# A four-layer decoder trunk on one core: norm weights as columns, norm scratch inside the mixers' memory, one unit of query weights kept for both tiles

## The chip, the cores and the metric

The kernel runs on one core of a Trainium2 chip. A core has a matrix engine (TensorE, PE in the profile), a vector engine (VectorE, DVE), an activation engine (ScalarE, ACT), a general engine (GpSimd, POOL) and a queue engine (SyncE, SP), all with their own instruction streams, and 16 DMA engines between HBM and the on-chip memory (SBUF). TensorE writes to a small accumulator memory (PSUM), in banks of 128 x 512 float32. The metric is the device time of one execution in microseconds. Everything is float32.

## The reference, cut to what matters

256 tokens of width 1024 pass four layers. Each layer adds a token mixer (HGRN2, forgetting attention, Mamba-2 SSD, HGRN2) and then a PEER feed-forward: a product-key lookup that picks, for each token and each of 8 heads, 16 of 16384 experts, reads one row of `u` and one of `v` for each, and sums.

```python
def rmsnorm(x, g, eps=NORM_EPS):
    y = x * lax.rsqrt(jnp.mean(x * x, axis=-1, keepdims=True) + eps)
    return y * g

for i in range(DEPTH):
    h = h + mixer[i](rmsnorm(h, norm_mix[i]))
    h = h + peer_ffn(rmsnorm(h, norm_ffn[i]), peer_w_q[i], peer_keys[i], peer_u[i], peer_v[i])
return rmsnorm(h, norm_final)

def peer_ffn(xb, w_q, sub_keys, u_tab, v_tab):            # a block of 128 tokens
    q = (xb @ w_q).reshape(M, 8, 2, 128)                  # 16 score blocks, top 16 of each, top 16 of the sums
    ...
    act = gelu(einsum('md,mhkd->mhk', xb, u_tab[idx])) * gates
    return einsum('mhk,mhkd->md', act, v_tab[idx])
```

So there are eight norms of 256 tokens with weights of their own before mixers and feed-forwards, and a ninth at the end. `norm_ffn(h)` is used twice: for the queries, and for the products with the gathered `u` rows.

## The kernel before, in words

The tokens are two tiles of 128 (t = 0, 1), so that a layer and a tile make a stage: STAGES = 8. The expert part of stage s runs together with the mixer, the norms and the queries of stage s + 1 ("side work").

**The expert part.** A stage has 64 steps (loop `for i in range(64 * s, 64 * s + 64)`). A step takes two gathers, each an indirect DMA issued by POOL (L1096 in `fetch`) that brings 128 rows of 2048 floats (u and v of one expert, 8 KB) into one of eight buffers `GB` in the tile `arena`. `dot` multiplies the u half with `XR` on DVE and sums it, `spread` makes a gelu and diagonal weights `dg` on ACT, and TensorE adds the v half into `acc` (L1125). After that the buffer is free and POOL may issue the gather eight places further on. `XR` holds the normed tokens 64 at a time, each twice down the partitions; `repeated` makes it once per stage, with four matmuls against a selection matrix `sel` (at step 62), which ACT and DVE copy out of PSUM at step 63 (L1204, L1213, `copy` beside it).

**The side work** is a generator that gives out pieces, one piece in a step, as long as a count of estimated cost lies under SIDE[s] times the step's number over 56. Its weights come in units of 128 x 2048 floats (1 MB) through three buffers `raw`. `load_to` (L267) puts the loads on SP in the order of use, up to three units ahead, and a load waits until TensorE is done with the unit that held its buffer. A stage with HGRN2 uses 20 units, attention 16, SSD 32, and each stage then 8 units of query weights `wq`. The second tile of a layer loads all units again.

**The norm** (`normed`): ACT squares and sums, DVE and ACT make the reciprocal root r, DVE computes `xn = h * r * nw` (in `scale`), TensorE turns `xn` into `xT` (features on partitions; helper `turn`, L237) and ACT copies it from PSUM (L405). `nw` is one row of 1024 weights, copied to all 128 partitions by a DMA on SP (`norm_load`, L251): 512 KB on the chip's side. The next row is loaded in `scale`, after the last use of the row before. `xn` and `nw` are regions of `arena` of their own.

**Helpers.** Matmuls are recorded under L233 (`mm`) and L237 (`turn`), all DVE work of the wrapper `vec` under L198, activations under L211. One float32 matmul in the code is two records of TensorE in the profile.

Of the kernel before, what the change touches and what calls it, by code (L numbers as in the profile page):

```python
# [9 lines left out]
F32 = mybir.dt.float32  # L10
# [4 lines left out]
OP = mybir.AluOpType  # L15
AX = mybir.AxisListType

P = 128
T = 256
D = 1024  # L20
DC = D // P
DEPTH = 4
EPS = 1e-6
UNIT = 2048
# [4 lines left out]
NRAW = 3  # L29
MIX = 14560  # L30
STAGES = 2 * DEPTH
KIND = ("hg", "fox", "ssd", "hg")

SIDE = (37.8, 34.6, 37.5, 100, 100, 38.6, 38.4, 1.8)
# [57 lines left out]
def _cols(v):  # L92
    return np.ascontiguousarray(v.reshape(-1, P).T)
# [12 lines left out]
def _layout(x, norm_mix, norm_ffn, norm_final, hgrn_lb_logits, hgrn_w_in, hgrn_gnorm, hgrn_w_out,  # L106
            fox_w_in, fox_b_f, fox_w_out, ssm_w_in, ssm_conv_w, ssm_conv_b, ssm_dt_bias, ssm_a_log,
            ssm_d, ssm_gnorm, ssm_w_out, peer_w_q, peer_keys, peer_u, peer_v):
    a = {}
    a["x"] = np.ascontiguousarray(x.reshape(2, P, D))  # L110
    a["norms"] = np.ascontiguousarray(np.concatenate([norm_mix, norm_ffn, norm_final[None]], axis=0))

    def cols(w, *cuts):
        return np.concatenate([w[:, c * 512:(c + 1) * 512] for c in cuts], axis=1)

    for j in range(2):

        a[f"hg{j}"] = np.concatenate([_in_units(cols(hgrn_w_in[j], 2, 3, 0, 1, 4, 5, 6, 7)), _out_units(hgrn_w_out[j])])

    w = fox_w_in[0]  # L120
    a["fox"] = np.concatenate([_in_units(cols(w, 4, 5, 0, 2, 1, 3)), _out_units(fox_w_out[0])])

    w2 = ssm_w_in[0]
    a["ssm"] = np.concatenate([_in_units(cols(w2, 8, 10, 4, 5, 9, 11, 6, 7, 0, 1, 2, 3)), _out_units(ssm_w_out[0])])
    for i in range(DEPTH):
        a["wq%d" % i] = _in_units(peer_w_q[i])

    def small(m):
        m = np.concatenate([m, np.zeros((m.shape[0], 32 - m.shape[1]), m.dtype)], axis=1)
        return np.ascontiguousarray(m.reshape(DC, P, 32).transpose(1, 0, 2)).reshape(P, DC * 32)  # L130

    a["keys"] = np.ascontiguousarray(peer_keys.transpose(0, 4, 1, 2, 3)).reshape(DEPTH, P, UNIT)
    a["uv"] = np.concatenate([peer_u.reshape(-1, D), peer_v.reshape(-1, D)], axis=1)
    a["gn"] = np.ascontiguousarray(hgrn_gnorm)
    parts = [
        ("wf", small(w[:, 3072:3088])), ("wdt", small(w2[:, 6144:6176])),
        ("lbl", np.ascontiguousarray(hgrn_lb_logits.reshape(DEPTH, 8, P).transpose(2, 1, 0)).reshape(P, 32)),
        ("bf", _rows(fox_b_f[0])), ("dtb", _rows(ssm_dt_bias[0])), ("alog", _rows(ssm_a_log[0])),
        ("cw", np.ascontiguousarray(ssm_conv_w[0].reshape(4, 32, P).transpose(2, 1, 0)).reshape(P, 128)),
        ("cb", _cols(ssm_conv_b[0])), ("sg", _cols(ssm_gnorm[0])),  # L140
        ("sd", _cols(np.repeat(ssm_d[0], 64))),
    ]
    off = 0
    for name, arr in parts:
        PARAMS[name] = (off, arr.shape[1])
        off += arr.shape[1]
    a["par"] = np.ascontiguousarray(np.concatenate([q for _, q in parts], axis=1))
    a["const"] = _constants()
    for name in ("hg0", "fox", "ssm"):
        UNITS[name[:3].rstrip("0")] = a[name].shape[0]  # L150
    return a
# [8 lines left out]
def trunk(ctx: ExitStack, tc: tile.TileContext, d: dict, out: bass.AP):  # L160
    nc = tc.nc
    SB = bass.MemoryType.PSUM
    cpool = ctx.enter_context(tc.tile_pool(name="c", bufs=1))
# [8 lines left out]
    npar = sum(n for _, n in PARAMS.values())  # L172
    cst = cpool.tile([P, ncst], F32, name="cst")
    par = cpool.tile([P, npar], F32, name="par")
    sizes = (("h", 2 * D), ("xn", D), ("nw", D), ("xT", D), ("XR", 2 * D), ("keys", UNIT), ("SS", 2048), ("mix", MIX),
             ("gb", NGB * 2 * D))
    arena = cpool.tile([P, sum(n for _, n in sizes)], F32, name="arena")
    at_, o_ = {}, 0
# [1 line left out]
        at_[name] = arena[:, o_:o_ + n]  # L180
        o_ += n
    h = at_["h"].rearrange("p (t n) -> p t n", t=2)
    xn, nw = at_["xn"], at_["nw"]
    xT = at_["xT"].rearrange("p (c t) -> p c t", c=DC)
    XR = at_["XR"].rearrange("p (g n) -> p g n", g=2)
    keys = at_["keys"].rearrange("p (g k) -> p g k", g=16)
# [2 lines left out]
    mix = at_["mix"]  # L189
# [11 lines left out]
    vec = Vector()  # L201
# [15 lines left out]
    def PR(name):  # L217
        o, n = PARAMS[name]
        return par[:, o:o + n]
# [4 lines left out]
    spare = cpool.tile([P, 1], F32, name="spare")  # L224
    trimask = cpool.tile([P, 4, P], U8, name="trimask")
    m64 = cpool.tile([P, 64], F32, name="m64")
    sel = cpool.tile([P, 2, 2, 64], F32, name="sel")

    pe = [0.0]

    def mm(o, w, m, start, stop):
        pe[0] += max(0.27, 0.0017 * m.free_size())
        nc.tensor.matmul(o, w, m, start=start, stop=stop)  # L233
# [13 lines left out]
    def bank():  # L247
        return psp.tile([P, 512], F32, name="ps")

    def norm_load(row):  # L250
        nc.sync.dma_start(nw, d["norms"][row:row + 1].to_broadcast([P, D]))  # L251


    stream = []
    for l in range(DEPTH):
        nm = ("hg%d" % (l // 3), "fox", "ssm", "hg%d" % (l // 3))[l]
        for t in range(2):
            stream += [(nm, i) for i in range(UNITS[KIND[l] if KIND[l] != "ssd" else "ssm"])]
            stream += [("wq%d" % l, i) for i in range(8)]
    raws = {}  # L260
    pos = [0, 0]

    def load_to(n):
        while pos[0] < min(n, len(stream)):
            nm, i = stream[pos[0]]
            r = rawp.tile([P, UNIT], F32, name="raw")
            nc.sync.dma_start(r, d[nm][i])  # L267
            raws[pos[0]] = r
            pos[0] += 1

# [50 lines left out]
    def slot(*fs):  # L321
        for f in fs:
            f()
        yield
        flush()
        yield
# [33 lines left out]
    def turned(src, use, n=4):  # L360

        b = bank().rearrange("p (c t) -> p c t", c=4)
        for c in range(n):
            turn(b[:, c], src[:, c * P:(c + 1) * P])
        later(lambda: use(b))


    def normed(t, acc, row, to_x=True, alone=False):

        st = wk2.tile([P, 4], F32, name="st")  # L370
        es = [slice(e * 512, (e + 1) * 512) for e in range(2)]
        r = st[:, 2:3]

        def add(e):
            tm(h[:, t, es[e]], acc[e], h[:, t, es[e]], op=OP.add)

        def square(e):
            act(xn[:, es[e]], h[:, t, es[e]], AF.Square, accum_out=st[:, e:e + 1])

        def root():  # L380
            tm(r, st[:, 0:1], st[:, 1:2], op=OP.add)
            act(r, r, AF.Sqrt, scale=1.0 / D, bias=eps)

        def scale():
            assert rows.pop(0) == row
            vec.reciprocal(r, r)
            for e in range(2):
                stt(xn[:, es[e]], h[:, t, es[e]], r, nw[:, es[e]], op0=OP.mult, op1=OP.mult)
                if not to_x:
                    nc.sync.dma_start(out[t * P:(t + 1) * P, es[e]], xn[:, es[e]])  # L390
            if rows and rows[0] != row:
                norm_load(rows[0])

        both = [lambda e=e: square(e) for e in range(2)]
        if acc is not None:
            adds = [lambda e=e: add(e) for e in range(2)]
            if alone:
                yield from slot(lambda: deferred.extend(adds))
            else:
                both = [adds[0], both[0], adds[1], both[1]]  # L400
        yield from slot(lambda: deferred.extend(both))
        for f in (root, scale):
            yield from slot(lambda: later(f))
        if to_x:
            yield from slot(*(lambda q=q: turned(xn[:, es[q]], lambda b: nc.scalar.copy(xT[:, 4 * q:4 * q + 4], b))  # L405
                              for q in range(2)))


    def hgrn(l, t, carry):
# [669 lines left out]
    def repeated():  # L1079

        todo = []
        for g in range(2):
            for e in range(2):
                b = bank()
                mm(b, sel[:, g].rearrange("p j i -> p (j i)"), xn[:, e * 512:(e + 1) * 512], True, True)
                todo.append((XR[:, g, e * 512:(e + 1) * 512], b))
        return todo

# [42 lines left out]
    def ready(s, acc):  # L1131

        l, t = s // 2, s % 2
        carry = {}
        yield from normed(t, acc, l, alone=True)
        if t == 0:
            nc.sync.dma_start(keys, d["keys"][l].rearrange("p (g k) -> p g k", g=16))
        yield from mixers[KIND[l]](l, t, carry)
        yield from normed(t, carry["acc"], DEPTH + l)
        yield from queries(s)  # L1140

    def side(s):

        if s + 1 < STAGES:
            yield from ready(s + 1, accs.pop(s - 1) if s else None)
        else:
            yield from normed(0, accs.pop(s - 1), 2 * DEPTH, False, alone=True)


    nc.sync.dma_start(h[:, 0], d["x"][0])  # L1150
    nc.sync.dma_start(cst, d["const"])
    nc.sync.dma_start(par, d["par"])
    nc.vector.memset(eps, EPS)
    rows = [r for s in range(STAGES) for r in (s // 2, DEPTH + s // 2)] + [2 * DEPTH] * 2
    first = ready(0, None)
    norm_load(rows[0])
    for _ in range(2):
        next(first)
    load_to(NRAW)
    nc.sync.dma_start(h[:, 1], d["x"][1])  # L1160
    nc.vector.tensor_copy(trimask, tri[:, None, :].to_broadcast([P, 4, P]))
    tm(m64, ident[:, 0:64], ident[:, 64:P], op=OP.add)
    for g in range(2):
        nc.vector.tensor_copy(sel[:, g], ident[:, None, g * 64:g * 64 + 64].to_broadcast([P, 2, 64]))
    while (0, 0) not in scored:
        next(first)
    while (0, 0) not in got:
# [6 lines left out]
    for s in range(STAGES):  # L1174
# [51 lines left out]
        others()  # L1226
        for _ in work:
            pass
    for _ in normed(1, accs.pop(STAGES - 1), 2 * DEPTH, False):
        pass  # L1230


# [13 lines left out]
```

## Time and profile before

| | us |
|---|---|
| median of 3 runs (3303.47 to 3305.14) | 3303.48 |
| the profiled execution, its own time | 3302.7 |
| its span, first to last instruction | 3300.7 |
| TensorE / VectorE / ScalarE / GpSimd busy | 2500.2 / 2109.8 / 1368.9 / 1182.8 |

The span is cut into 40 slices of 82.5 us in the page. A digit of a slice is the busy share in tenths, GB/s what all DMA queues moved in it. Queue q0 carries the gathers that POOL issues, queue q1 all that SP issues. TensorE's busy time is modelled, so that its share is no measure of how near to its limit it is.

### The profile page before, as it was taken

The page shows a single profiled execution, that of the slowest core. Times are in us where ns is not written, and L with a number is a line of the kernel's source. Part 1 is how long each engine was busy: PE and PEld are TensorE (multiplying, and loading weights), DVE is VectorE, ACT ScalarE, POOL GpSimd, SP SyncE. Part 2 cuts the span into 40 slices and gives each one's busy share as a digit, 9 for nine tenths or more (in the row PEclk, how much of TensorE's full clock was granted, in tenths as well). Part 3 has the DMA queues.
Part 4 walks back from the last instruction along what each step waited for, and adds up shares of the span by engine and source line. Part 5 has one row for each costly group of instructions (what it writes and reads, how often), then busy time and mean ns, then how long its engine had stood idle before and what let it go on. Part 6 is the DMA issues. An engine that isn't in the chain of part 4 may idle for free.

```text
span 3300.7 us, 30061 instructions
## 1 busy us (share of the span) xinstructions
PE 2500.2 (76%) x8202; PEld 1090.8 (33%) x8202; DVE 2109.8 (64%) x5545; ACT 1368.9 (41%) x3911; POOL 1182.8 (36%) x1030
## 2 busy tenths in 40 slices
PE   8887776777677776788877897878777787775555
PEld 4433332332333332343333453323333333332222
DVE  1367657576565756688656886576665666567764
ACT  3254333254243533476334674244443543333332
POOL 0133334334343334333333333343333333344442
PEclk9989988898889898999988998889988898888777
DMA  7799999999999999999999999999999999999998
GB/s 269 268 421 421 421 421 420 421 411 420 418 410 421 392 421 421 421 421 419 415 419 409 419 419 417 419 411 421 418 414 413 416 420 420 414 406 412 419 415 331
DMA packets 186645, 1343.88 MB, mean 407 GB/s; under 512 B 20720, under 2 KB 20976, under 8 KB 24176
## 3 DMA queue, kind: packets, MB, share of 16 engines
q0 software_dynamic: 147456, 1073.81, 78.8%
q1 hardware_dynamic: 39024, 268.17, 19.9%
q8 instruction: 68, 1.11, 0.1%
q14 instruction: 97, 0.79, 0.1%
HBM read 1340.84 MB, written 1.05 MB: 407 GB/s over the span
## 4 chain that ended last, share of the span: by engine, by line
DMA 57%; PE 17%; issue 9%; DVE 9%; ACT 4%; POOL 3%; POOLq 0%; SPq 0%; DVEq 0%; ACTq 0%
DMA arena<-in_uv,ix 56%; PE acc L1125 9%; DVE arena L198 8%; PE pj L233 5%; POOL arena L1096 3%; PE ps L233 3%; ACT dots L211 2%; ACT L211 1%; ACT dg L211 1%; PE ps L237 1%; ACT arena L211 0%; DVE ti L198 0%; DMA raw<-in_wq 0%; DVE eq L198 0%; DVE ts L198 0%
## 5 line engine op out<-in xcount | busy, mean ns | idle before, releaser
L198 DVE SCALAR_TENSOR_TENSOR arena<-arena 128x1024 f32<-128x1024 f32 (+3 forms) x1282 | 1321.4, 1047 | 976.2 <-DMA arena<-in_uv,ix 930.1
L1096 POOL DMA_INDIRECT arena<-in_uv,ix x1024 | 1180.7, 1153 | 2090.8 <-PE acc L1125 1524.7
L1125 PE MATMUL acc<-arena,dg 128*64 128x512 f32 x4096 | 1315.1, 728 | 765.2 <-ACT dg L211 748.3
L1125 PEld LDWEIGHTS acc<-arena,dg 128*64 128x64 f32 x4096 | 484.8, 155 | 1405.9 <-ACT dg L211 1065.3
L233 PE MATMUL pj<-raw,arena 128*128 128x512 f32 x1920 | 905.9, 615 | 5.5 <-DMA raw<-in_wq 1.5
L211 ACT ACTIVATE dots<-dots 128x2 f32<-128x2 f32 x512 | 103.5, 202 | 1663.7 <-DVE arena L198 1662.6
L233 PEld LDWEIGHTS pj<-raw,arena 128*128 128x128 f32 x1920 | 355.0, 195 | 566.9 <-issue 552.8
L211 ACT ACT_TABLE_LOAD x326 | 418.3, 1283 | 5.8 <-PEq L1238 0.7
L211 ACT ACTIVATE dg<-m,dots 128x64 f32<-128x64 f32 x1024 | 292.5, 333 | 0.0
L211 ACT ACTIVATE dots<-dots,gs 128x1 f32<-128x1 f32 x1024 | 245.6, 286 | 16.8
L233 PE MATMUL ps<-arena 128*128 128x128 f32 (+5 forms) x1040 | 127.5, 284 | 1.4 <-ACT arena L972 1.4
L233 PEld LDWEIGHTS ps<-arena 128*128 128x128 f32 (+3 forms) x1040 | 103.0, 166 | 74.9 <-issue 55.6
L237 PE MATMUL ps<-cst,arena 128*128 128x128 f32 x560 | 93.1, 296 | 19.5 <-DVE arena L198 16.2
L237 PEld LDWEIGHTS ps<-cst,arena 128*128 128x128 f32 x560 | 68.7, 151 | 99.3 <-issue 36.1
L211 ACT ACTIVATE arena<-arena 128x512 f32<-128x512 f32 (+3 forms) x132 | 67.7, 555 | 44.4 <-DVE arena L198 41.7
L198 DVE DVE_READ_ACCUMULATOR arena<-arena 128x1 f32 x1024 | 83.7, 82 | 0.0
L233 PE MATMUL ps<-cst,arena 128*128 128x128 f32 (+3 forms) x352 | 74.2, 344 | 0.0
L198 DVE MAX8 sv<-arena 128x8 f32<-128x128 f32 x256 | 61.6, 282 | 13.9 <-ACT arena L981 13.9
L198 DVE FIND_INDEX8 si<-sv,arena 128x8 uint32<-128x128 f32 x256 | 69.7, 284 | 0.0
L211 ACT ACTIVATE arena<-ps 128x512 f32<-128x512 f32 (+4 forms) x113 | 46.5, 458 | 28.3 <-PE ps L233 27.7
L233 PEld LDWEIGHTS ps<-cst,arena 128*128 128x128 f32 x352 | 50.4, 193 | 22.9 <-issue 13.3
L198 DVE COPY gs<-ig 64x16 f32<-64x16 f32 x256 | 54.3, 212 | 4.7
(102 smaller groups left out, 1101.7 us busy)
## 6 DMA issues: line engine op xcount, KB each, us to landing
raw<-in_hg SPq DMA_DIRECT2D x80, 1024.0 KB
raw<-in_wq SPq DMA_DIRECT2D x64, 1024.0 KB
raw<-in_ssm SPq DMA_DIRECT2D x64, 1024.0 KB
raw<-in_fox SPq DMA_DIRECT2D x32, 1024.0 KB
arena<-in_uv,ix POOLq DMA_INDIRECT x1024
arena<-in_norms SPq DMA_DIRECT2D x17, 512.0 KB
arena<-in_keys SPq DMA_DIRECT2D x4, 1024.0 KB
arena<-in_x SPq DMA_DIRECT2D x2, 512.0 KB
```

What stands on the lines that cost most here:

```text
L198: return getattr(nc.vector, name)(o, *a, **k)
L211: nc.scalar.activation(o, i, f, **k)
L233: nc.tensor.matmul(o, w, m, start=start, stop=stop)
L237: nc.tensor.transpose(o, i, ident)
L1096: nc.gpsimd.indirect_dma_start(GB[n % NGB], None, d["uv"], bass.IndirectOffsetOnAxis(ap=got[s, hh][0][:, g, q:q + 1], axis=0))
L1125: nc.tensor.matmul(accs[s][e][g * 64:g * 64 + 64], dg[:, g], v, start=hh == 0 and q == 0, stop=hh == 7 and q == NQ - 1)
```

## The change

1. The rows of weights of the eight inner norms are laid out as 8 columns each (feature on partition) in the parameter tile `par`, which grows from 832 to 896 columns. `norm_load` is gone. DVE computes `xn = h * r` alone, and the weights are multiplied in when the turned norm leaves PSUM: a DVE multiplication with a broadcast column (`weighed`) in place of ACT's copy. The final norm keeps a row of weights, loaded once into the mixers' memory.
2. `xn` no longer has a region of its own; it lies in a part of the mixers' memory `mix` that is not in use at the time of a norm (`FREE`).
3. Since `xn` now lacks the weights, `repeated` makes `XR` from `xT`: for each of four banks, eight matmuls with 64 columns of `xT` as the stationary operand and the identity as the moving one.
4. The first unit of each layer's `wq` goes to a region `kept` (as large as `xn` and `nw` were together) and is loaded for the first tile alone.

```diff
+NKEPT = 1
+FREE = {"hg": 0, "fox": 64 + 8 * T + 2 * D, "ssd": 352 + 16 * T + 96 + D}
...
-    sizes = (("h", 2 * D), ("xn", D), ("nw", D), ("xT", D), ("XR", 2 * D), ("keys", UNIT), ("SS", 2048), ("mix", MIX),
+    sizes = (("h", 2 * D), ("xT", D), ("XR", 2 * D), ("keys", UNIT), ("SS", 2048), ("mix", MIX), ("kept", NKEPT * UNIT),
...
-    def norm_load(row):
-        nc.sync.dma_start(nw, d["norms"][row:row + 1].to_broadcast([P, D]))
...
             nm, i = stream[pos[0]]
-            r = rawp.tile([P, UNIT], F32, name="raw")
-            nc.sync.dma_start(r, d[nm][i])
+            keep = nm[0] == "w" and i < NKEPT
+            r = at_["kept"][:, i * UNIT:(i + 1) * UNIT] if keep else rawp.tile([P, UNIT], F32, name="raw")
+            if not keep or (nm, i) not in kept:
+                nc.sync.dma_start(r, d[nm][i])
+            if keep:
+                kept.add((nm, i))
...
         def scale():
-            assert rows.pop(0) == row
             vec.reciprocal(r, r)
             for e in range(2):
-                stt(xn[:, es[e]], h[:, t, es[e]], r, nw[:, es[e]], op0=OP.mult, op1=OP.mult)
-                if not to_x:
+                if last:
+                    stt(xn[:, es[e]], h[:, t, es[e]], r, row[:, es[e]], op0=OP.mult, op1=OP.mult)
                     nc.sync.dma_start(out[t * P:(t + 1) * P, es[e]], xn[:, es[e]])
-            if rows and rows[0] != row:
-                norm_load(rows[0])
-
+                else:
+                    vec.tensor_scalar(xn[:, es[e]], h[:, t, es[e]], r, None, op0=OP.mult)
+
+        def weighed(q, b):
+            c = slice(4 * q, 4 * q + 4)
+            tm(xT[:, c], b, PR("nw")[:, 8 * row + 4 * q:8 * row + 4 * q + 4].unsqueeze(2).to_broadcast([P, 4, P]), op=OP.mult)
...
-            yield from slot(*(lambda q=q: turned(xn[:, es[q]], lambda b: nc.scalar.copy(xT[:, 4 * q:4 * q + 4], b))
-                              for q in range(2)))
+            yield from slot(*(lambda q=q: turned(xn[:, es[q]], lambda b: weighed(q, b)) for q in range(2)))
...
                 b = bank()
-                mm(b, sel[:, g].rearrange("p j i -> p (j i)"), xn[:, e * 512:(e + 1) * 512], True, True)
+                for c in range(4):
+                    for j in range(2):
+                        mm(b[j * 64:j * 64 + 64, c * P:(c + 1) * P], xT[:, 4 * e + c, g * 64:g * 64 + 64], ident, True, True)
```

The order of SP's queue at the program's start and through the first layer, before (`in_norms` are the rows of norm weights, `in_hg` and `in_wq` the units):

```order
L1152 DMA par<-in_par 128x832
L251 DMA arena<-in_norms 128x1024
L267 DMA raw<-in_hg 128x2048 x3
L1160 DMA arena<-in_x 128x1024
L251 DMA arena<-in_norms 128x1024
L1137 DMA arena<-in_keys 128x2048
```

and now:

```order
L1165 DMA par<-in_par 128x896
L270 DMA raw<-in_hg 128x2048 x3
L1171 DMA arena<-in_x 128x1024
L1149 DMA arena<-in_keys 128x2048
```

Further on in the same queue, the end of the first layer's first tile and its whole second tile, before:

```order
L267 DMA raw<-in_wq 128x2048 x3
L251 DMA arena<-in_norms 128x1024
L267 DMA raw<-in_wq 128x2048 x5
L267 DMA raw<-in_hg 128x2048 x3
L251 DMA arena<-in_norms 128x1024
L267 DMA raw<-in_hg 128x2048 x17
L267 DMA raw<-in_wq 128x2048 x3
L251 DMA arena<-in_norms 128x1024
L267 DMA raw<-in_wq 128x2048 x5
```

and now, with `arena<-in_wq` the load into `kept`:

```order
L270 DMA arena<-in_wq 128x2048
L270 DMA raw<-in_wq 128x2048 x7
L270 DMA raw<-in_hg 128x2048 x20
L270 DMA raw<-in_wq 128x2048 x7
```

The loads of norm weights are gone, the second tile loads seven units of `in_wq` where it loaded eight, and the other loads stand in the same order.

On TensorE, the change from one stage's expert part to the next (here the first one; `acc` are the experts' sums), before:

```order
L1125 MATMUL acc<-arena,dg 64x512 x28
L233 MATMUL ps<-arena,sel 128x512 x4
L1125 MATMUL acc<-arena,dg 64x512 x20
```

and now:

```order
L1136 MATMUL acc<-arena,dg 64x512 x28
L235 MATMUL ps<-cst,arena 64x128 x32
L1136 MATMUL acc<-arena,dg 64x512 x20
```

The four matmuls of `repeated` have become 32, at the same place in the queue.

On DVE, the first norm that runs beside experts (second layer-one tile), before:

```order
L198 RECIPROCAL st<-st 128x1
L198 SCALAR_TENSOR_TENSOR arena<-arena,st 128x512 x2
L198 SCALAR_TENSOR_TENSOR arena,dots<-arena 128x1024 x2
L198 TENSOR_TENSOR eq<-cst,af 128x512
L198 TENSOR_TENSOR eq<-eq,sf 128x512
L198 TENSOR_REDUCE af<-eq 128x32
L198 TENSOR_SCALAR sf<-af 128x16
L198 TENSOR_TENSOR ig<-sf,af 128x16
L198 SCALAR_TENSOR_TENSOR arena,dots<-arena 128x1024 x2
```

and now:

```order
L201 RECIPROCAL st<-st 128x1
L201 TENSOR_SCALAR arena<-arena,st 128x512 x2
L201 SCALAR_TENSOR_TENSOR arena,dots<-arena 128x1024 x2
L201 TENSOR_TENSOR eq<-cst,af 128x512
L201 TENSOR_TENSOR eq<-eq,sf 128x512
L201 TENSOR_REDUCE af<-eq 128x32
L201 TENSOR_SCALAR sf<-af 128x16
L201 TENSOR_TENSOR ig<-sf,af 128x16
L201 TENSOR_TENSOR arena<-ps,par 128x512 x2
L201 SCALAR_TENSOR_TENSOR arena,dots<-arena 128x1024 x2
```

The scaling has one tensor operand in place of two, and two multiplications out of PSUM stand behind it, ahead of the next two products with gathered rows.

## Rows read from the trace of the kernel before

**Rows 1.** The page: engines, 40 slices, DMA queues.
```profile
PE 2500.2 (76%) x8202; PEld 1090.8 (33%) x8202; DVE 2109.8 (64%) x5545; ACT 1368.9 (41%) x3911; POOL 1182.8 (36%) x1030
...
DMA  7799999999999999999999999999999999999998
GB/s 269 268 421 421 421 421 420 421 411 420 418 410 421 392 421 421 421 421 419 415 419 409 419 419 417 419 411 421 418 414 413 416 420 420 414 406 412 419 415 331
...
q0 software_dynamic: 147456, 1073.81, 78.8%
q1 hardware_dynamic: 39024, 268.17, 19.9%
```

**Rows 2.** The page, the chain that ended last, by engine.
```profile
DMA 57%; PE 17%; issue 9%; DVE 9%; ACT 4%; POOL 3%; POOLq 0%; SPq 0%; DVEq 0%; ACTq 0%
```

**Rows 3.** Windows: stretch, length, busy time of each engine, granted clock, DMA share, GB/s.
```profile
140.00:540.00 400.00, 299.41 (x972) 128.20 (x970) 252.64 (x672) 161.00 (x454) 145.72 (x126) 0.89 1.01 421
...
940.00:1330.00 390.00, 290.18 (x1004) 130.19 (x1006) 256.54 (x685) 160.12 (x483) 150.85 (x130) 0.90 1.00 413
...
2970.00:3280.00 310.00, 182.28 (x491) 71.11 (x492) 206.64 (x505) 93.57 (x346) 135.45 (x122) 0.79 1.01 416
```

**Rows 4.** Waits: engine, line, waited for, us in total, times, longest.
```profile
POOL arena L1096 <- PE acc L1125: 1524.7, 441, 18.4
...
DVE arena L198 <- DMA arena<-in_uv,ix: 930.1, 559, 8.2
```

**Rows 5.** DMA issues by line: names, count, size of each.
```profile
raw<-in_wq SPq DMA_DIRECT2D x64, 1024.0 KB
...
arena<-in_norms SPq DMA_DIRECT2D x17, 512.0 KB
```

**Rows 6.** SP in order of time, 100 to 180 us: start, length, line, names.
```profile
111.41 0.33 SPq L251 DMA_DIRECT2D arena<-in_norms  x1
...
174.00 0.33 SPq L251 DMA_DIRECT2D arena<-in_norms  x1
```

**Rows 7.** The chain of the first 40 us in order of time: start, length, what.
```profile
2.13 6.94 DMA arena<-in_norms
...
9.20 0.76 DVE arena L198
...
24.28 7.36 DMA raw<-in_hg
```

**Rows 8.** VectorE in order of time, 0 to 12 us; idle time ahead in brackets.
```profile
7.54 0.16 DVE L198 RECIPROCAL st<-st 128x1 f32<-128x1 f32 x1 [0.36 <-ACT st L211]
9.20 1.41 DVE L198 SCALAR_TENSOR_TENSOR arena<-arena,st 128x512 f32<-128x512 f32 x2 [1.49 <-DMA arena<-in_norms]
```

**Rows 9.** Groups by shape: count, busy us, mean ns of one, idle before, releaser.
```profile
L198 DVE SCALAR_TENSOR_TENSOR arena<-arena,st 128x512 f32<-128x512 f32 x36 | 25.4, 748 | 2.2 <-DMA arena<-in_norms 1.5
L198 DVE TENSOR_TENSOR arena<-ps,arena 128x512 f32<-128x512 f32 x16 | 10.9, 683 | 20.2 <-PE ps L237 20.2
L198 DVE TENSOR_SCALAR arena<-arena,fst 128x256 f32<-128x256 f32 x16 | 5.2, 370 | 0.3
L198 DVE TENSOR_SCALAR arena<-arena,fst 128x128 f32<-128x128 f32 x16 | 3.9, 283 | 0.3
```

**Rows 10.** TensorE in order of time, three stretches.
```profile
2960.30 3.92 PE L1125 MATMUL acc<-arena,dg 128*64 128x512 f32 x8 [1.05 <-ACT dg L211]
2964.15 3.98 PE L233 MATMUL ps<-arena,sel 128*128 128x512 f32 x8
...
2973.37 2.17 PE L1125 MATMUL acc<-arena,dg 128*64 128x512 f32 x8 [3.27 <-ACT dg L211]
...
1519.99 0.44 PE L233 MATMUL ps<-arena 128*64 128x128 f32 x4
...
41.66 0.60 PE L237 MATMUL ps<-cst,arena 128*128 128x128 f32 x4
```

**Rows 11.** VectorE and GpSimd at the last change of stage.
```profile
2968.16 0.69 DVE L198 COPY arena<-ps 128x512 f32<-128x512 f32 x1 [3.94 <-PE ps L233]
...
2983.62 1.23 DVE L198 SCALAR_TENSOR_TENSOR arena<-arena 128x1024 f32<-128x1024 f32 x1 [1.28 <-DMA arena<-in_uv,ix]
...
2971.50 1.64 POOL L1096 DMA_INDIRECT arena<-in_uv,ix  x1 [0.30 <-issue]
```

**Rows 12.** Windows around the last change of stage, columns as in rows 3.
```profile
2960.00:2970.00 10.00, 9.70 (x24) 3.93 (x24) 4.35 (x8) 3.19 (x11) 3.03 (x4) 0.76 0.98 367
2970.00:2980.00 10.00, 4.45 (x17) 1.86 (x16) 9.97 (x31) 2.48 (x11) 5.72 (x5) 1.00 0.94 348
```

More of the change, by code (lines that the diff above doesn't have):

```diff
@@ L110, in _layout @@
     a["x"] = np.ascontiguousarray(x.reshape(2, P, D))
-    a["norms"] = np.ascontiguousarray(np.concatenate([norm_mix, norm_ffn, norm_final[None]], axis=0))
+    a["last"] = np.ascontiguousarray(norm_final[None])
     def cols(w, *cuts):
@@ L141, in _layout @@
         ("sd", _cols(np.repeat(ssm_d[0], 64))),
+        ("nw", np.concatenate([_cols(v) for v in (*norm_mix, *norm_ffn)], axis=1)),
     ]
@@ L182, in trunk @@
     h = at_["h"].rearrange("p (t n) -> p t n", t=2)
-    xn, nw = at_["xn"], at_["nw"]
     xT = at_["xT"].rearrange("p (c t) -> p c t", c=DC)
@@ L226, in trunk @@
     m64 = cpool.tile([P, 64], F32, name="m64")
-    sel = cpool.tile([P, 2, 2, 64], F32, name="sel")
     pe = [0.0]
@@ L260, in trunk @@
     raws = {}
+    kept = set()
     pos = [0, 0]
@@ L365, in turned, with normed @@
         later(lambda: use(b))
-    def normed(t, acc, row, to_x=True, alone=False):
+    def normed(t, acc, row, xn, alone=False):
         st = wk2.tile([P, 4], F32, name="st")
@@ L384, in scale @@
         def scale():
-            assert rows.pop(0) == row
             vec.reciprocal(r, r)
             for e in range(2):
-                stt(xn[:, es[e]], h[:, t, es[e]], r, nw[:, es[e]], op0=OP.mult, op1=OP.mult)
-                if not to_x:
+                if last:
+                    stt(xn[:, es[e]], h[:, t, es[e]], r, row[:, es[e]], op0=OP.mult, op1=OP.mult)
                     nc.sync.dma_start(out[t * P:(t + 1) * P, es[e]], xn[:, es[e]])
-            if rows and rows[0] != row:
-                norm_load(rows[0])
+                else:
[3 more added lines that the diff above has]
+            tm(xT[:, c], b, PR("nw")[:, 8 * row + 4 * q:8 * row + 4 * q + 4].unsqueeze(2).to_broadcast([P, 4, P]), op=OP.mult)
+        last = not isinstance(row, int)
         both = [lambda e=e: square(e) for e in range(2)]
@@ L403, in normed @@
             yield from slot(lambda: later(f))
-        if to_x:
-            yield from slot(*(lambda q=q: turned(xn[:, es[q]], lambda b: nc.scalar.copy(xT[:, 4 * q:4 * q + 4], b))
-                              for q in range(2)))
+        if not last:
+            yield from slot(*(lambda q=q: turned(xn[:, es[q]], lambda b: weighed(q, b)) for q in range(2)))
     def hgrn(l, t, carry):
@@ L1134, in ready @@
         carry = {}
-        yield from normed(t, acc, l, alone=True)
+        xn = mix[:, FREE[KIND[l]]:FREE[KIND[l]] + D]
+        yield from normed(t, acc, l, xn, alone=True)
         if t == 0:
@@ L1138, in ready @@
         yield from mixers[KIND[l]](l, t, carry)
-        yield from normed(t, carry["acc"], DEPTH + l)
+        yield from normed(t, carry["acc"], DEPTH + l, xn)
         yield from queries(s)
@@ L1146, in side @@
         else:
-            yield from normed(0, accs.pop(s - 1), 2 * DEPTH, False, alone=True)
+            nc.sync.dma_start(mix[:, 0:D], d["last"].to_broadcast([P, D]))
+            yield from normed(0, accs.pop(s - 1), mix[:, 0:D], mix[:, D:2 * D], alone=True)
     nc.sync.dma_start(h[:, 0], d["x"][0])
@@ L1153, in trunk @@
     nc.vector.memset(eps, EPS)
-    rows = [r for s in range(STAGES) for r in (s // 2, DEPTH + s // 2)] + [2 * DEPTH] * 2
     first = ready(0, None)
-    norm_load(rows[0])
     for _ in range(2):
@@ L1162, in trunk @@
     tm(m64, ident[:, 0:64], ident[:, 64:P], op=OP.add)
-    for g in range(2):
-        nc.vector.tensor_copy(sel[:, g], ident[:, None, g * 64:g * 64 + 64].to_broadcast([P, 2, 64]))
     while (0, 0) not in scored:
@@ L1228, in trunk @@
             pass
-    for _ in normed(1, accs.pop(STAGES - 1), 2 * DEPTH, False):
+    for _ in normed(1, accs.pop(STAGES - 1), mix[:, 0:D], mix[:, 2 * D:3 * D]):
         pass
```

## The prediction, made before the changed kernel ran

> **What bounds the kernel now.** I read the slices of the page first. The busiest engine, TensorE, shows 76%, but from the third slice to the last but one the DMA engines stand at 9 and move 392 to 421 GB/s [rows 1]. The windows by stage say it more finely: DMA share 1.00 or 1.01 in the first, the weakest and the last stage, at 421, 413 and 416 GB/s [rows 3]. The last of them loads almost no weights, so gathers alone fill the DMA engines nearly as well as gathers mixed with weights. Then the chain: 57% of the span is DMA [rows 2]. The waits fit: VectorE waits 930 us for gathered rows, and POOL waits 1525 us for TensorE to free a buffer [rows 4]. The latter looks like a limit by buffers, but POOL refills a queue that is not empty: a gather issued at 2971.50 is first used at 2983.62 [rows 11], 12 us later, and one gather of 1.05 MB at 420 GB/s takes 2.5 us; so four to five gathers are in the queue. Hence from about 140 us, when that state begins, to 3280 us the time is bytes over rate, and a byte not moved is time saved. Outside that stretch the first 140 us count by their own chain, and the tail of some 20 us is not touched.
>
> **The bytes.** The page counts 17 loads of norm rows at 512 KB (0.524 MB) and 64 units of query weights at 1024 KB (1.049 MB) [rows 5]. SP's first three norm loads fall before 140 us, the third at 111.41; the fourth is at 174.00 [rows 6]. So 14 lie in the full stretch; one load for the final norm is added there, which leaves 13 x 0.524 = 6.82 MB. Of the query weights the second tile of each layer loads one unit less: 4 x 1.049 = 4.19 MB; SP's order shows just that, and no load that comes instead. Together 11.01 MB. At 417 GB/s, between the stages' 413 and 421, that is 26.4 us (26.2 at 421, 26.7 at 413). `par` grows by 128 x 64 x 4 bytes, 0.03 MB, under 0.1 us.
>
> **The start.** The chain begins with the first norm row: issued at 2.13, 6.94 us [rows 7]. VectorE has its reciprocal at 7.70 (7.54 + 0.16) and then stands 1.49 us for that row [rows 8]. Without it the scaling starts 1.5 us earlier. Behind it TensorE runs on the first units until it waits for a unit whose load takes 7.36 us from 24.28 on [rows 7]. Two norm rows, 1.05 MB or 2.5 us of DMA, no longer lie ahead of that unit. So TensorE comes 1.5 us earlier and the unit up to 2.5 us earlier. I take 2 us; the ends are 0 (something behind, such as the first routing, absorbs it) and 3.5 (both add up).
>
> **VectorE and ScalarE in the norms.** There are 16 inner norms. Each drops two scalings of 748 ns and gets two with one tensor operand. The trace has these at 128 x 128 and 128 x 256, at 283 and 370 ns [rows 9]; 87 ns for 128 more columns gives some 545 ns at 512 (an estimate). It also gets two multiplications from PSUM at 683 ns [rows 9]. That is 2 x (545 + 683 - 748) = 0.96 us more per norm, 15 us in all, on an engine busy for 2110 of 3301 us and waiting 930 us for gathers; ScalarE loses two copies per norm. What stands behind the two multiplications in VectorE's queue are two products with gathered rows; they start up to 1.4 us late, and a buffer comes free that much later, against 12 us of queued gathers. I count 0; if nothing covered it, 15 us. The estimate of cost that paces the side work rises by under 1% (its formula counts a piece by TensorE or VectorE, whichever is more, and at least 0.5), so the side work keeps its steps.
>
> **The change of stage.** `repeated` now takes 64 records of 128 columns in place of 8 of 512. Before, they took 3.98 us at the last change, and VectorE stood 3.94 us for the last bank [rows 10, 11], with the products of the next stage behind it. What 64-column matmuls cost is seen in the SSD mixer: four records of 128 columns, two matmuls into the two halves of the partitions, take 0.44 us end to end [rows 10]; that is not a pace yet, since the last record drains in it. Bounds: if the halves do not overlap, 64 records at the pace of turns (four in 0.60 us with the drain, so at most 0.15 each) take up to 9.6 us; if they overlap fully, 32 times 0.11 (3.98/8/4, a quarter of the old record plus drain) gives 3.5 us, about what it was. The nearest row is the pair of the same shape: 16 pairs at 0.3 to 0.44 us, 5 to 7 us. So the copy to `XR` comes 1 to 3 us later at each of the seven changes that run beside gathers. The DMA queue's 12 us hide this, but not wholly: around the change the rate already dips, 367 and 348 GB/s at shares of 0.98 and 0.94 [rows 12]. I take 0.3 us each, 2 us in all; ends 0 and 7 x 5.7 = 40.
>
> At this place the Trainium skill has a rule (TensorEngine Tiling (Array Packing), Theoretical Speedup): a stationary operand of at most 64 columns lets two such matmuls run side by side, up to twice as fast. The row of the SSD pair agrees in part: four records took less than four turns, 0.44 against 0.60 us. By that rule at its best the term would be 0 and the sum 2 us lower.
>
> **Sum.** 3302.7 - 26.4 - 2 + 0 + 2 = 3276.3 us for an execution like the profiled one. The median of the runs lies 0.8 us above that one's own time, so 3277 us.
>
> **Rivals.**
> (a) *Paced by buffers.* If POOL's wait for TensorE [rows 4] is what limits in the stretches without weights, a norm load that falls there used DMA time that nobody else takes. For it: the dip to 348 GB/s [rows 12] and 413 GB/s in the attention stage [rows 3]. Against it: shares of 1.00 and more over whole stages. If half of the bytes saved bring nothing, the gain of 26.4 halves: 3277 + 13 = 3290 us.
> (b) *VectorE blocks POOL.* POOL issues every gather, and 32 scalings with a single tensor operand on VectorE are new. If each held POOL up for its whole 0.545 us and that showed, 32 x 0.545 = 17 us come back: 3294 us. Against it: POOL is busy for 36% [rows 1] and runs 12 us ahead. The Trainium skill names this mechanism (SBUF — State Buffer, Who interferes with whom): a one-source float32 operation on SBUF may take the port that GpSimd needs to write descriptors, and GpSimd then waits for its end. No row here shows such a wait.
> (c) *Slower: the change of stage runs the DMA queue dry.* The mechanism is the 64 records at half the clock. The eight records of the experts' sums take 3.92 us at 2960.30 and 2.17 at 2973.37 [rows 10], with a granted clock of 0.76 and 1.00 in the windows around them [rows 12], so nearly such a factor occurs. Without overlap they would take 2 x 9.6 = 19 us, 15 more than now; all seven would cost 107 us if nothing hid them. It decides when more than 28/7 = 4 us per change show, so only if the delay passes 12 + 4 us, which needs the slow end of both bounds. With 6 us shown at each, 3277 - 2 + 42 = 3317 us.
> (d) *More than the bytes.* If the dips of the rate stem from the norm rows among the gathers, up to 10 us more go: 3267 us.
> That the loads stay is excluded by SP's order.
>
> **How the numbers follow.** Forecast 3277: 0.76. (a) 0.12, (b) 0.04, (c) 0.04, (d) 0.04. The likeliest case's own range is 3270 to 3285 (start 0 to 3.5, change of stage 0 to 8, rate). For 8 in 10 I go to 3266 below, which takes in (d), and to 3292 above, which takes in most of (a). About 0.2%, 6.6 us, is what a measurement of this kernel tells from no change; faster by more is under 3296.9 us. Forecast, (a), most of (b) and (d) are there: 0.91. Within it lie the rest of (b) and the mild half of (c): 0.05. Slower 0.04.
>
> **What would show it.** DMA bytes 12.5 MB lower (1343.9 to 1331.3), the share still 9 in all slices but the ends, the rate within 410 to 421, and the last gather some 26 us earlier: each step right. The stages' lengths should shrink by 2.6 to 5.0 us in second-tile mixers' stages (two norm rows and a unit) and 2.5 us in the others. The first scaling should start at about 7.7 us. Wrong: `repeated` over 7 us with a DMA share under 0.9 behind it (c); a lower rate in stretches without weights (a); POOL's spans longer beside the new scalings (b).

## The result, and the profile after

The changed kernel takes 3275.1 us (median of 6 runs, 3273.0 to 3277.48) against 3303.6 us (6 runs, 3302.36 to 3305.14): the ratio is 0.9914, 95% interval 0.9901 to 0.9926. The forecast was 3277 us. The profiled execution lies at the upper end of its runs, 3277.4 us, 2.3 us above their median. The two traces differ by some 25 us and the medians by 28.5, so what is read from the traces below accounts for 25 us; where the other 3 lie is not shown (the start, below, is a candidate).

The page of the changed kernel, the lines that answer to [rows 1] and [rows 2]:

```profile
span 3275.6 us, 30941 instructions
...
PE 2498.5 (76%) x8650; PEld 1114.0 (34%) x8650; DVE 2116.8 (65%) x5575; ACT 1354.9 (41%) x3879; POOL 1181.0 (36%) x1030
...
DMA  7699999999999999999999999999999999999998
GB/s 259 249 421 421 421 421 420 421 414 417 420 405 421 415 417 418 413 420 416 408 420 406 421 420 407 420 412 421 417 418 417 404 421 421 420 409 419 416 414 338
DMA packets 183769, 1331.40 MB, mean 406 GB/s; under 512 B 20400, under 2 KB 20656, under 8 KB 21808
...
q1 hardware_dynamic: 36144, 255.61, 19.1%
...
DMA 58%; PE 13%; DVE 11%; issue 10%; ACT 4%; POOL 3%; POOLq 0%; DVEq 0%; ACTq 0%
```

Engines and gather queue are as they were. Queue q1 moves 255.61 MB where it moved 268.17, and the DMA digits are still 9 from the third slice on. Windows by stage, columns as in [rows 3] (the last stage is moved by the time won):

```profile
140.00:540.00 400.00, 305.11 (x978) 129.74 (x976) 254.70 (x677) 160.60 (x453) 143.95 (x128) 0.89 1.01 421
940.00:1330.00 390.00, 296.34 (x1069) 136.25 (x1071) 259.93 (x695) 161.44 (x489) 146.36 (x132) 0.89 1.01 416
2950.00:3255.00 305.00, 181.32 (x481) 70.06 (x480) 201.51 (x488) 91.84 (x339) 130.59 (x120) 0.78 1.01 417
```

Share and rate are the same or a little above those of before. So the same engines, at the same rate, carry fewer bytes. How long that stretch is can be read from the first and the last gather, in the view of one line (minimum, median and maximum in ns, then first and last start in us). Before:

```profile
L1096 POOL DMA_INDIRECT arena<-in_uv,ix x1024: 932/939/2621, 134.5 to 3272.9; - x171
```

and after:

```profile
L1107 POOL DMA_INDIRECT arena<-in_uv,ix x1024: 932/941/2626, 136.4 to 3249.0; - x171
```

From first to last gather 3138.4 us have become 3112.6, which is 25.8 us less. The first gather is 1.9 us later, and from the last gather to the end of the span 27.8 us have become 26.6. Together: -25.8 + 1.9 - 1.2 = -25.1 us, the spans' 3300.7 - 3275.6.

### The profile page after: what moved, and what is told of

Read it like the earlier page. It is cut to its first block, busy times and chain, and to the rows that moved or that the text cites. A ratio compares the mean times of both kernels' runs of the same rounds, so it can differ in the third digit from the quotient of the medians.

```text
span 3275.6 us, 30941 instructions
## 1 busy us (share of the span) xinstructions
PE 2498.5 (76%) x8650; PEld 1114.0 (34%) x8650; DVE 2116.8 (65%) x5575; ACT 1354.9 (41%) x3879; POOL 1181.0 (36%) x1030
## 2 busy tenths in 40 slices
DMA packets 183769, 1331.40 MB, mean 406 GB/s; under 512 B 20400, under 2 KB 20656, under 8 KB 21808
## 3 DMA queue, kind: packets, MB, share of 16 engines
q1 hardware_dynamic: 36144, 255.61, 19.1%
## 4 chain that ended last, share of the span: by engine, by line
DMA 58%; PE 13%; DVE 11%; issue 10%; ACT 4%; POOL 3%; POOLq 0%; DVEq 0%; ACTq 0%
DMA arena<-in_uv,ix 57%; DVE arena L201 8%; PE acc L1136 7%; PE pj L235 4%; POOL arena L1107 3%; PE ps L235 2%; ACT dots L214 2%; ACT L214 1%; ACT dg L214 1%; ACT arena L214 1%; PE ps L239 1%; DVE eq L201 1%; DVE af L201 0%; DVE ti L201 0%; DMA raw<-in_hg 0%
## 5 line engine op out<-in xcount | busy, mean ns | idle before, releaser
L1107 POOL DMA_INDIRECT arena<-in_uv,ix x1024 | 1178.9, 1151 | 2068.7 <-PE acc L1136 1492.7
L235 PE MATMUL pj<-raw,arena 128*128 128x512 f32 x1856 | 871.5, 613 | 5.2 <-DMA raw<-in_ssm 2.7
L235 PEld LDWEIGHTS pj<-raw,arena 128*128 128x128 f32 x1856 | 340.9, 194 | 537.7 <-issue 516.5
L235 PE MATMUL ps<-cst,arena 128*64 128x128 f32 (+4 forms) x864 | 107.8, 310 | 0.0
L239 PEld LDWEIGHTS ps<-cst,arena 128*128 128x128 f32 x560 | 67.2, 148 | 99.4 <-issue 43.3
L235 PEld LDWEIGHTS ps<-cst,arena 128*64 128x64 f32 (+1 forms) x864 | 84.2, 165 | 27.4 <-issue 16.7
L214 ACT ACTIVATE arena<-ps 128x512 f32<-128x512 f32 (+4 forms) x113 | 46.5, 458 | 28.4 <-PE ps L235 27.8
```

Source lines behind the costliest of these rows:

```text
L214: nc.scalar.activation(o, i, f, **k)
L239: nc.tensor.transpose(o, i, ident)
L1107: nc.gpsimd.indirect_dma_start(GB[n % NGB], None, d["uv"], bass.IndirectOffsetOnAxis(ap=got[s, hh][0][:, g, q:q + 1], axis=0))
```

## The experiments

Two theories stood against each other. "Bytes": from the first gathers on the DMA engines are full and time is bytes over rate. "Waits": what was won is SP's queue without the norm loads, which waited for VectorE and stood ahead of the weights, or the new order of work. Ratios are against the kernel before, run beside each; it took 3302.0 to 3303.4 us there (medians) and 3303.6 beside the changed kernel, so a difference between kernels of different sessions is good to some 2 us.

**e1, without the kept unit.**

```diff
-NKEPT = 1
+NKEPT = 0
```

> The changed kernel without the kept unit: the second tile loads all eight units of query weights again, the norms stay as changed. Theory 'bytes' (from 140 us on the DMA engines are full, so time = bytes over rate): 4 x 1.049 MB come back at 417 GB/s, 10.1 us, so 3275 + 10 = 3285 us. Rival 'waits' (what was won is SP's queue without norm loads that block it, and the other engines' order): the kept unit is worth little, 3275 to 3278 us.

Measured: 3284.63 us, ratio 0.9948 (0.9934 to 0.9962). That is 9.5 us over the changed kernel, for 4.19 MB, as "bytes" said.

**e2, the norm rows loaded again and read by nobody.**

```diff
...
+            if not last:
+                nc.sync.dma_start(at_["kept"][:, 0:D], d["norms"][row:row + 1].to_broadcast([P, D]))
```

> As e1, and each of the 16 inner norms again loads a row of weights to all partitions (512 KB, by SP, at the place in the order where the kernel before had it), into a region that nobody reads and without a wait for VectorE. All compute work is that of the changed kernel. Theory 'bytes': 14 of the loads lie in the full stretch, 14 x 0.524 MB at 417 GB/s = 17.6 us on top of e1, so 3303 us, the time before. Rival 'waits': nobody waits for these loads, so the time of e1.

Measured: 3301.6 us, ratio 0.9997 (0.9988 to 1.0006): 17.0 us over e1, where 17.6 were expected, and the time of the kernel before, though all compute work is the new one and no instruction waits for these loads. Its page shows the old total:

```profile
DMA packets 186649, 1343.98 MB, mean 407 GB/s; under 512 B 20720, under 2 KB 20976, under 8 KB 24176
```

With the bytes back the whole gain is gone, so the new order of work on the engines is not what won it. As the loads stand in SP's queue again too, e3 takes the bytes out and leaves the queue.

**e3, the kernel before with short norm rows.**

```diff
...
-        nc.sync.dma_start(nw, d["norms"][row:row + 1].to_broadcast([P, D]))
+        n = 128 if short else D
+        short.append(row)
+        nc.sync.dma_start(nw[:, 0:n], d["norms"][row:row + 1, 0:n].to_broadcast([P, n]))
```

> The kernel before, but the norm loads after the first bring only 128 of the 1024 weights (64 KB in place of 512 KB), with the same waits on both sides; the other weights stay those of the first row, so the output is not the reference's. Theory 'bytes': 15 loads in the full stretch (14 inner ones and the final row) x 0.459 MB at 417 GB/s = 16.5 us less, 3287 us. Rival 'waits': the waits are all there, 3303 us.

Measured: 3289.42 us, ratio 0.996 (0.9946 to 0.9973): 14 us less than before, with the waits in place. How long SP stands at these loads until VectorE is done with the row before (total us, times, longest) is in the kernel before

```profile
SPq L251 <- DVE arena L198: 634.4, 16, 79.5
```

and in e3's trace 627.3 us, also 16 times. "Waits" said no gain. "Bytes" said 16.5, for 15 loads; e3's trace has 14 behind 140 us (13 inner ones and the final row), which makes 15.4, and the interval of some 4 us either side holds both.

**e4, the 32 matmuls of `repeated` twice.**

```diff
-                for c in range(4):
+                for c in list(range(4)) * 2:
```

> The changed kernel, but at each change of stage the 32 matmuls that spread the normed tokens are done twice into the same banks, so that TensorE takes about 7.5 us there in place of 3.8 and the copies come 3.7 us later. Theory 'the DMA queue hides it' (12 us of gathers are queued): 3275 + 0 to 4 us. Rival 'each us at the change of stage shows': 7 x 3.7 = 26 us more, 3301 us.

Measured: 3276.53 us, ratio 0.9918 (0.9904 to 0.9932), so 1.4 us over the changed kernel, which is less than the intervals can tell from nothing. TensorE at the last change of stage in this kernel (the last 2 of the 128 records end at 2948.02):

```profile
2940.63 7.17 PE L235 MATMUL ps<-cst,arena 128*64 128x128 f32 x126
```

and in the changed kernel:

```profile
2938.85 3.89 PE L235 MATMUL ps<-cst,arena 128*64 128x128 f32 x64
```

Seven times some 3.5 us more on TensorE, with VectorE's next products behind it, cost 1.4 us by the medians. In the one trace, first to last gather takes 3118.2 us (134.1 to 3252.3), 5.6 more than in the changed kernel, so up to a quarter of the added work may show; the rival's whole is excluded. That the gathers already queued hide the rest is the likely reason; it was not measured by itself.

**e5, seven gather buffers in place of eight.**

```diff
-NGB = 8
+NGB = 7
```

> The changed kernel with seven gather buffers in place of eight, nothing else. One gather less is queued, 2.5 of some 12 us. Theory 'bytes' (the queue is deeper than it has to be): 3275 to 3280 us. Rival 'paced by buffers' (POOL's wait for TensorE is what limits): the same cycle now brings seven gathers where it brought eight, so the rate falls towards 7/8 wherever gathers stand alone; if half of the stretch is so paced, 3275 + 3130/2/7 = some 3500 us, and anything over 3300 us speaks for it.

Measured: 3275.55 us, ratio 0.9921 (0.9908 to 0.9935): no change. POOL waits for TensorE as long as ever (1515.5 us against 1492.7 in the changed kernel). So that wait, POOL's largest in total, does not set the pace here. Rival (a) of the prediction falls.

**e6, two kept units in the memory of the eighth buffer.**

```diff
-NGB = 8
+NGB = 7
-NKEPT = 1
+NKEPT = 2
```

> Two units of query weights kept, in the memory of the eighth gather buffer. Theory 'bytes': 10.1 us less than e5, so 3265 to 3270 us. Rival 'paced by buffers': above 3290 us.

Measured: 3264.28 us, ratio 0.9885 (0.987 to 0.99): 11.3 us less than e5, for 4.19 MB, as "bytes" said again.

**e7, two kept units in the memory of the third weight buffer.**

```diff
-NRAW = 3
+NRAW = 2
-NKEPT = 1
+NKEPT = 2
```

> Two units kept, in the memory of the third weight buffer; eight gather buffers. Theory 'bytes': 10.1 us less than the changed kernel, 3265 us, as long as weights arrive in time with two units ahead; a unit of 1 MB behind four to five gathers lands some 9 us after its issue. Rival 'weights come late': side work slips, the stages end with forced pieces, over 3275 us.

Measured: 3280.11 us, ratio 0.9935 (0.9921 to 0.9948). It moves as few bytes as e6 and takes 16 us longer, so the rival holds: weights come late. TensorE's largest groups in this kernel:

```profile
L235 PE MATMUL pj<-raw,arena 128*128 128x512 f32 x1792 | 863.5, 625 | 54.5 <-DMA raw<-in_ssm 27.2 <-DMA raw<-in_hg 16.8 <-DMA raw<-in_wq 9.8
```

and in the changed kernel:

```profile
L235 PE MATMUL pj<-raw,arena 128*128 128x512 f32 x1856 | 871.5, 613 | 5.2 <-DMA raw<-in_ssm 2.7 <-DMA raw<-in_hg 1.4 <-ACT arena L571 0.7
```

TensorE stands 54.5 us ahead of these matmuls, nearly all of it for weights and ten times as long. Part of the loss lies ahead of the full stretch: the first gather comes at 139.5 us, in e6 at 134.0. Two slices of e7's page stand at 381 and 383 GB/s, where the changed kernel has none between the second and the last below 404.

**e8, three kept units in the memory of two gather buffers.**

```diff
-NGB = 8
+NGB = 6
-NKEPT = 1
+NKEPT = 3
```

> Three units kept in the memory of two gather buffers. Theory 'bytes': 20.1 us less than the changed kernel, 3255 us, if six buffers still keep the queue from running dry (six buffers are 15 us of transfer, and a pair of buffers is in use some 5 to 6 us after it landed). Rival: the queue runs dry at each change of stage and in busy stages, 3275 us or more.

Measured: 3356.13 us, ratio 1.0169 (1.0151 to 1.0187): slower than before with 21 MB less. The last stage of this kernel, without weights to load:

```profile
2990.00:3320.00 330.00, 195.34 (x503) 74.10 (x499) 203.69 (x498) 92.72 (x338) 135.11 (x120) 0.74 0.98 379
```

and the same part of the changed kernel:

```profile
2990.00:3240.00 250.00, 150.38 (x397) 56.80 (x393) 165.98 (x402) 75.82 (x278) 107.74 (x99) 0.77 1.01 416
```

The DMA share is still 0.98 but the rate is 379 GB/s. A share near 1 is thus not enough to call the transfers the limit; with two buffers fewer, and no weights that could come late, the buffers pace them.

**e9, the norms' new work on VectorE twice.**

```diff
                     vec.tensor_scalar(xn[:, es[e]], h[:, t, es[e]], r, None, op0=OP.mult)
+                    nc.vector.tensor_scalar(xn[:, es[e]], h[:, t, es[e]], r, None, op0=OP.mult)
...
             tm(xT[:, c], b, PR("nw")[:, ...].unsqueeze(2).to_broadcast([P, 4, P]), op=OP.mult)
+            nc.vector.tensor_tensor(xT[:, c], b, PR("nw")[:, ...].unsqueeze(2).to_broadcast([P, 4, P]), op=OP.mult)
```

> The changed kernel, but VectorE does each of the 32 new scalings (489 ns) and each of the 32 new multiplications out of PSUM (682 ns) twice, to the same result: 37 us more work on VectorE, and 32 more one-source scalings beside GpSimd's gathers. The count that paces the side work is not told of it. Theory 'hidden under the transfers': 3275 us, at most 3278. Rival 'VectorE's work, or its hold on GpSimd, shows': with all of it 3312 us, with half 3294 us.

Measured: 3279.27 us, ratio 0.9934 (0.9921 to 0.9948). Of 37 us of added work 4.2 show by the medians (some 6 by the ratios), one more than the theory's upper end; the two intervals overlap, so the size of that rest is open, but half of 37 is excluded. The traces say where it may lie: first to last gather takes 3113.6 us in e9's (136.5 to 3250.1) and 3112.6 in the changed kernel's, so beside the gathers about 1 us shows in these two executions. Two of the 16 norms come before the first gather, with no gathers to hide them.

**e10, e6 and a third unit kept in the attention layer alone.**

```diff
-            keep = nm[0] == "w" and i < NKEPT
+            keep = nm[0] == "w" and i < NKEPT + (nm == "wq1")
...
+            r = mix[:, 10432:10432 + UNIT] if keep and i == NKEPT else at_["kept"][:, i * UNIT:(i + 1) * UNIT] if keep else ...
```

> As e6 (two kept units, seven gather buffers), and the attention layer keeps a third unit of query weights in a part of the mixers' memory that it does not use. One load of 1.049 MB less. Theory 'bytes': 2.5 us less than e6, 3262 us. Rival: no further gain, 3264 us.

Measured: 3260.77 us, ratio 0.9877 (0.9862 to 0.9892), the fastest here. The step from e6 is 3.5 us where 2.5 were expected, but the intervals overlap, so it is not resolved.

## Why the prediction was right, point by point

**The bytes, -26.4 us: right.** From first to last gather the traces differ by 25.8 us. e2 gives the whole back, e3 takes the norm rows' part and keeps SP's waits, e1 gives the kept unit's part. Per MB: 9.5 us for 4.19 (e1), 17.0 for 7.34 (e2), 11.3 for 4.19 (e6), so 2.3 to 2.7 us, where 1 MB at 417 GB/s is 2.4.

**The start, -2 us: wrong in the step "the unit up to 2.5 us earlier".** In the profiled execution the first gather comes 1.9 us later, not 2 us earlier. The scaling is earlier nearly as forecast: it starts at 7.95, before at 9.20, which is 1.25 of the 1.5 us. The chain of the first 40 us after, answering to [rows 7]:

```profile
7.75 0.17 DVE st L201
...
7.95 0.50 DVE arena L201
...
16.12 8.17 DMA raw<-in_hg
...
24.33 10.57 PE pj L235 x24
34.90 3.01 PE ps L235 x8
```

The unit that the prediction names, issued at 24.28 in the kernel before, is the sixth, and TensorE stood only 0.33 us for it:

```profile
31.68 3.70 PE L233 MATMUL pj<-raw,arena 128*128 128x512 f32 x8 [0.33 <-DMA raw<-in_hg]
...
35.39 3.01 PE ps L233 x8
```

In the changed kernel TensorE waits 1.37 us, and for the fourth unit. What its issue waited for was not the norm rows but its buffer: SP issues it when TensorE is done with the first unit, at 16.12, before at 17.41. So it could be issued only 1.3 us earlier, and it then took 8.17 us. The load of `keys` still lay ahead of it until some 18.8 us (issued at 4.52, 14.3 us to landing); what else made it slow was not tried. TensorE's next group starts at 34.90 in place of 35.39: 0.5 us are won there, and at 95.85 in place of 96.34 still the same 0.5.

Then TensorE itself is slower. The last units of the first mixer (24 records) and the first units of query weights (16) in the chain of the kernel before:

```profile
96.34 10.32 PE pj L233 x24
...
112.62 7.94 PE pj L233 x16
```

and of the changed kernel:

```profile
95.85 12.01 PE pj L235 x24
...
113.75 8.63 PE pj L235 x16
```

They take 1.69 and 0.69 us longer, 2.4 together; less the 0.5 won before, that is the 1.9 us by which the first gather is late. The granted clock fits. Windows of the kernel before:

```profile
95.00:100.00 5.00, 4.29 (x13) 2.21 (x14) 0.57 (x1) 0.58 (x1) 0.00 (x0) 1.00 0.50 198
110.00:115.00 5.00, 4.23 (x12) 2.53 (x13) 1.38 (x2) 1.17 (x2) 0.00 (x0) 0.66 0.50 174
115.00:120.00 5.00, 5.00 (x13) 2.09 (x11) 0.00 (x0) 0.00 (x0) 0.00 (x0) 1.00 0.33 108
```

and of the changed kernel:

```profile
95.00:100.00 5.00, 4.77 (x11) 2.26 (x12) 0.08 (x1) 0.59 (x1) 0.00 (x0) 0.66 0.92 387
110.00:115.00 5.00, 3.22 (x10) 2.38 (x11) 2.43 (x5) 0.99 (x2) 0.00 (x0) 0.50 0.37 157
115.00:120.00 5.00, 5.00 (x10) 2.03 (x10) 0.00 (x0) 0.00 (x0) 0.00 (x0) 0.82 0.00 0
```

The granted clock (third number from the right, the mean of a window) is 0.66, 0.50 and 0.82 where it was 1.00, 0.66 and 1.00. 1.00 is the level of 2.4 GHz and 0.50 that of 1.2 GHz; the other values are windows in which both occur. TensorE had stood idle for about the same time ahead of the first of these windows, 2.09 us until 95.23 and before 2.08 until 95.71.

How much of the start is luck of one execution shows in the other traces. In e1's trace the first gather comes at 132.9 us, 1.6 earlier than before:

```profile
L1107 POOL DMA_INDIRECT arena<-in_uv,ix x1024: 932/938/2625, 132.9 to 3254.4; - x171
```

and its windows are:

```profile
95.00:100.00 5.00, 5.00 (x13) 2.17 (x12) 0.00 (x0) 0.55 (x1) 0.00 (x0) 1.00 0.40 128
110.00:115.00 5.00, 5.00 (x13) 2.44 (x12) 1.38 (x2) 0.00 (x0) 0.00 (x0) 0.72 0.00 0
```

There the clock is 1.00 and 0.72 in those windows, and the two groups take 10.32 and 8.04 us, though the instructions up to about 94 us are the same as in the changed kernel. In e2, e4, e5, e6, e8 and e10, whose work up to the queries differs from the changed kernel's in a load or two at most, the first gather comes at 133.1 to 134.8 us. The profiled execution of the changed kernel, 136.4, is thus the latest of eight, and their median of 134.0 lies 0.5 us ahead of the one trace of the kernel before. What sets the clock in this stretch was not tried.

**The norms on ScalarE and VectorE, 0 us: right in size.** The two new forms, answering to [rows 9]:

```profile
L201 DVE TENSOR_TENSOR arena<-ps,par 128x512 f32<-128x512 f32 x32 | 20.7, 682 | 1.9 <-PE ps L239 1.9
L201 DVE TENSOR_SCALAR arena<-arena,st 128x512 f32<-128x512 f32 x32 | 14.3, 489 | 0.6
```

The scaling takes 489 ns, less than the 545 that were estimated, so a norm costs 2 x (489 + 682 - 748) = 0.85 us more on VectorE, 13.5 us in all. By e9's medians, 4.2 of 37, about 1.5 us of it may show.

**The change of stage, +2 us: too much.** The 64 records take 3.89 us at the last change (8 records took 3.98, [rows 10]). Over the seven changes beside gathers they take 3.78 to 3.89 us where the granted clock is 1.00 and up to 4.99 where it is 0.78; the 8 records took 3.70 to 4.08. VectorE waits for the last bank only 1.70 us there, against 3.94 [rows 11]:

```profile
2942.78 0.69 DVE L201 COPY arena<-ps 128x512 f32<-128x512 f32 x1 [1.70 <-PE ps L235]
```

The lower bound, two matmuls side by side, was the right end (its 0.11 us should read 0.12, 3.98/8/4, which makes 4.0 us and not 3.5), and the row of the SSD pair misled: its 0.44 us for four records held the drain of the last, which the prediction had noted. The Trainium skill's rule (TensorEngine Tiling (Array Packing), Theoretical Speedup), up to twice the speed for a stationary operand of at most 64 columns, is what the trace shows: 3.89 / 32 = 0.12 us for two records of 128 columns, as long as 128 columns of one old record took (3.98/8/4). e4 shows besides that even 3.5 us more would have counted little.

**The rivals.** (a) falls by e5 for eight and seven buffers; e8 shows that it is a real limit, at six. (b) is excluded as a large term by e9, which doubled the one-source scalings. (c) falls by e4. (d) is not borne out: the rate between 940 and 1330 us is 416 GB/s in e2, where the norm rows are back, and 413 in e3, where they are short, so the rows among the gathers are not what held it at 413.

**The sum.** The main term and its mechanism were right, but that the forecast comes so close is in part luck. In the profiled execution the start is 3.9 us off, and against it stand the change of stage, forecast some 2 us too dear, and 1.2 us at the end that nothing forecast.

**The signs.** The bytes (1331.40 MB, forecast 1331.3), the share and the first scaling came as named, and the last gather is 23.9 us earlier (forecast 26) because the start is late. The rate did not stay within 410 to 421 in the page's slices, which go down to 404 (before: 392). Nor do the stages shrink as named: between the starts of `repeated`'s matmuls they are 2.3, 5.7, 2.3, 5.2, 0.2, 3.4 and 8.0 us shorter, where 2.6 to 5.0 was named for the first, third, fifth and seventh (second-tile mixers) and 2.5 for the others. Only the sum, 27.2 us, came out as the bytes say; why it is spread otherwise was not tried.

## What to carry to other kernels

Where DMA engines are full and their queue holds several transfers, price a change in bytes at the measured rate and give the engines' own work little: here 2.3 to 2.7 us per MB, for norm rows and query weights alike, and some 4 of 37 us of added work on VectorE (e9). Spend on-chip memory where the queue's depth is more than it needs (the eighth gather buffer was worth nothing, a kept unit in its place 11 us), and find the edge by taking buffers away one at a time, since the next one, with a third kept unit in its place, cost 92 us against e6. A long wait of the issuing engine does not say that buffers are the limit; whether the rate falls with one buffer less does.

## What the runs showed of the hardware that was not expected

A DMA share of 0.98 went with 379 GB/s in e8, against 416 at 1.01: with two gather buffers fewer the engines counted as busy nearly as long and moved less, so that the share hides a shortage that the rate shows. The same lies in the start of the changed kernel: from 15 to 20 us the share is 1.02 at 348 GB/s, where the kernel before has 1.02 at 423. And 64-column matmuls that alternate between the two halves of the output partitions ran side by side, so that eight times the records with twice the columns in all (64 of 128 in place of 8 of 512) took TensorE 3.78 us where it had taken 3.70, both at a granted clock of 1.00.
